# Projection chunks in another order, and attention set between them at a computed rate, in a one-core decoder layer

## The chip, the cores and the metric

One core of one Trainium2 chip runs the whole program. The metric is the device time of one execution in microseconds; the median of three runs of the kernel before is 1526.23 us (1516.66 to 1528.02).

## The reference

One layer of a decoder with two kinds of mixer, over a prompt of 2048 tokens and 64 new (sample) tokens. All shapes below are for the prompt.

```python
u, va, za, q, k, vb, zb = split(rms_norm(x) @ w_in)          # w_in 1024 x 3584
q, k = rms_norm per head                                       # 8 heads x 64
# mixer A: 4 channel groups of 128, chunks of 128 positions
a = rms_norm(u * (tril(w_s) @ rms_norm(va) + b_s)) * silu(za)
# mixer B: three dilated window patterns, r = 1, 4, 16, 129 keys each
o_r, lse_r = softmax attention of t to t - j*r, j = 0..128
b = rms_norm(sum_r softmax(lse)_r * o_r) * silu(zb)
h = x + concat(a, b) @ w_out
y = h + sigmoid(h @ w_ple_gate) * rms_norm(p @ w_ple)
```

The sample tokens do the same against a cache of 2048 keys and values per sequence.

## The kernel before

The projection is cut by columns into eight chunks. A chunk "A i" holds u, va and za of channel group i (384 columns); a chunk "B i" holds q, k, vb and zb of the head pair i (512 columns). `order` (L1251) lists them as A0 B0 B1 A1 B2 B3 A2 A3. Each chunk is a loop over 16 prompt tiles of 128 tokens and one sample tile (j from 0 to 16, L1284); a prompt tile is 24 matmuls (`gemm`, L433; operands are split into float16 halves, three products each). ScalarE (ACT) and VectorE (DVE) empty the result from PSUM (`psg`, three buffers; L475 to L491 for B, L565 to L571 for A), and GpSimd (POOL) scales it (L500 to L513, L581, L582). While a chunk runs, the weights of the next are loaded and split (`wprep`, L333); in the last chunk those of the three final products are (`wprep3`, L799; the low halves are L831 on VectorE).

Attention of a head pair needs its B chunk. `attn` (L642) cuts a pair into units. The first half of a unit is `scores` (L688): matmuls L698 and L699 into `pss`, a masked maximum on VectorE (L704), an exponential on ScalarE (L712), the float16 split on VectorE (L715, L716) and a transposing DMA to `pT` (L718). The second half is `stage_c` (L721): matmuls L739 to L741 with the values, and a row tile `rec` written to DRAM (L748 to L752). When a pair's last unit is through, `combine` (L755) runs once for each quarter of the tokens: it loads the three patterns' rows (`rl`, L760; three buffers) and the gates (`gzl`, L763), weighs and adds them on GpSimd (L776, L778, L781, L790, L792) with small VectorE steps between, and writes `catd` (L794). The four quarters follow each other in the same three buffers, and all of them need the last rows of pattern 3. The pairs use one buffer for their keys and queries (`kq`, L346), so pair i begins when pair i-1 is done.

The units are set between the projection's matmuls by `Pump` (L55). `tick` is called after each two matmuls and adds their planned nanoseconds times `rate` to a credit; units, each with a planned cost, are set while the credit is positive. The rate is 0.6 in every chunk (L1280) and 0.5 in the final stage (L1357). A unit's second half is due 8000 planned ns after its first. Before half of a B chunk, `pump.run` (L1343) sets what is left of the pair before.

The samples' attention (`all_samples`, L1229, four rounds of `sample`, L1063) is handed over at the end of chunk B3 (L1338) and is set only when no unit of a pair is left (`_step`, L97). A round multiplies cached keys by queries on GpSimd (L1126, 16 times: tiles `K` loaded at L1122 and `qB` at L1125, in the three buffers each that `pT` and `pc` use in attention), sums them on VectorE (L1127), transposes other keys on TensorE (L1106, L1111), and weighs values with `L1187` and `L1206`.

The final stage goes through the 16 prompt tiles: `p3_load` reads `catd` (L891), `halves_T` (L845) scales and splits it (L839, L861, L863) and transposes it by DMA (`Tc`, L862, L864), and `gemm2` (L867) multiplies by w_out, w_ple and w_ple_gate (L874). Tile 0 needs the first quarter of `combine` of pair 3.

Every engine works off its own list in the order in which a scheduler has put it. All DMAs here but a few small ones are issued from the one list of SP.

Of the kernel before, what the change touches and what calls it, by code (L numbers as in the profile page):

```python
# [24 lines left out]
NT = T // P  # L25
# [18 lines left out]
W_V = 4000.0  # L44
W_V3 = 3000.0
QK_LAG = 3000.0
P_LAG = 8000.0
MIX_LAG = 12000.0

# [86 lines left out]
def tile_hymba_gmlp_dilated_attn_step(  # L136
# [30 lines left out]
    drm = ctx.enter_context(tc.tile_pool(name="drm", bufs=1, space=DRAM))  # L167
    pump = Pump(3, P_LAG)
    uid = [0]

    def nm(s):
        uid[0] += 1
        return f"{s}_{uid[0]}"
# [259 lines left out]
    def gemm(j, wt, ncol):  # L433
        g = pst("g", 3)
        n = 0
        for kt in range(KT):
            w = wt[kt // 2]
            a, b = w[:, kt % 2, 0, :ncol], w[:, kt % 2, 1, :ncol]
            lh = xT[j][:, kt]
            for l, r in ((lh, a), (lh, b), (xT[j][:, KT + kt], a)) if j < NT else ((lh, a), (lh, b)):  # L440
                last_mm[0] = nc.tensor.matmul(g[:, :ncol], lhsT=l, rhs=r, start=(n == 0),  # L441
                                              stop=(n == (23 if j < NT else 15)))
                n += 1
                if n % 2 == 0:
                    pump.tick(2 * (ncol * 0.416 + 5))
        return g if j < NT else fold(g, ncol, "tmpA")
# [27 lines left out]

    def b_evac(G, q, g, sc):  # L475
        m = G["m"]
        g4 = g[:m, 0:256].rearrange("p (a d) -> p a d", d=HD)
        nc.scalar.activation(G["raw"][:m, q, :], g[:m, 0:256], AF.Copy)
        sq = wk.tile([P, 256], F32, name=nm("sq"), tag="sq", bufs=2)
        nc.scalar.activation(sq[:m], g[:m, 0:256], AF.Square)  # L480
        nc.vector.tensor_reduce(G["ss"][:m, q * 4:(q + 1) * 4], sq[:m].rearrange("p (a d) -> p a d", d=HD),
                                axis=AX.X, op=ALU.add)
        if m == P:
            gv = g[:, 256:384].rearrange("p (h d) -> p h d", h=2)
            vh = G["vv"][:, q, :, 0:64]
            nc.scalar.activation(vh, gv, AF.Copy, scale=VS)
            nc.vector.scalar_tensor_tensor(G["vv"][:, q, :, 65:129], gv, VS, vh, op0=ALU.mult, op1=ALU.subtract)
        nc.scalar.activation(G["vo"][:m, q, :], g[:m, 256:384], AF.Copy, scale=sc[:m, 1:2])
# [148 lines left out]
    vt = {}  # L637

    done = {}
    v_open = []  # L640

    def attn(hp, sc, grp):  # L642
        start = pump.now + QK_LAG
        qk2 = kq[hp]
        Q, KH, KL = qk2[:, 0:2], qk2[:, 2:4], qk2[:, 4:6]
        steps = []
        if grp is None:
            for c in range(0, 16, 2):
                steps.append((3, c // 4, [(c % 4 + s, False, slice(c + s, T, 16), slice(c + s, T, 16))
                                          for s in range(2)]))  # L650
        else:
            n = grp
            for j in range(4 * n, 4 * n + 4):
                steps.append((1, n, [(j % 4, j > 0, slice(j * P, (j + 1) * P),
                                      slice(max(j - 1, 0) * P, (j + 1) * P))]))
            for c in range(4):
                steps.append((2, n, [(c, n > 0, slice(n * 512 + c, (n + 1) * 512, 4),
                                      slice(max(n - 1, 0) * 512 + c, (n + 1) * 512, 4))]))
        rec = {}
        for pat, g, sub in steps:  # L660
            o = {}

            def first(pat=pat, g=g, sub=sub, o=o):
                if sub[0][0] == 0:
                    if pat != 1:
                        vload(hp, pat, g)
                    rec[pat] = wk.tile([P, 4, 2, RW], F32, name=nm("rec"), tag="rec", bufs=2)
                o["r"] = rec[pat]
                o["pT"], cost = scores(Q, KH, KL, o["r"], sub)
                return cost  # L670

            def second(pat=pat, g=g, sub=sub, o=o):
                with behind():
                    cost = stage_c(hp, pat, g, sub, o["r"], o["pT"])
                if pat == 1 and (sub[0][0] == 0 and g or sub[0][0] == 3 and g == 3):
                    v_open.pop(0)
                return cost
            pump.unit(start, first, second)
        if grp is None:
            for jg in range(4):  # L680
                def comb(jg=jg):
                    combine(hp, jg, sc)
                    done[hp] = jg == 3
                    return 0.0
                pump.unit(start, comb, None)
# [562 lines left out]
            nc.vector.tensor_scalar(gch[:, 2, :], gch[:, 1, :], cS, None, op0=ALU.mult)  # L1248
        gains.append(gch)

    order = [("A", 0), ("B", 0), ("B", 1), ("A", 1), ("B", 2), ("B", 3), ("A", 2), ("A", 3)]  # L1251

    room = wk.tile([P, 6, D], F32, name="room", tag="qk2", bufs=1)
    xst = []
# [18 lines left out]
    for ci, (kind, i) in enumerate(order):  # L1273
# [10 lines left out]
        for j in range(NT + 1):  # L1284
# [25 lines left out]
            if j % 4 == 0:  # L1310
                mk = b_group if kind == "B" else a_group
                G = mk(i, j // 4, 4, P) if j < NT else mk(i, 4, 1, TS)
            g = gemm(j, wt, ncol)
            if ci + 1 < len(order):
                for _ in range(1 if ci else FIRST_PREP[j]):
# [103 lines left out]
```

## Time and profile before

| | |
|---|---|
| median of 3 runs | 1526.23 us |
| the profiled execution's own time | 1526.24 us |
| its span on the trace | 1524.5 us |
| TensorE (PE) busy | 1361.5 us, 89% |
| VectorE (DVE) busy | 1160.8 us, 76% |
| ScalarE (ACT) busy | 725.9 us, 48% |
| GpSimd (POOL) busy | 538.1 us, 35% |
| mean granted TensorE clock | 0.959 |

An engine's share is a mean over nine stages that have different limits, so it says little alone. The trace can be asked for the busy time of each engine in given stretches, for instructions in order of time, and for groups of instructions by line.

### The profile page before, as it was taken

To read this page: it belongs to the slowest core of one execution; us is meant where nothing else is said; L and a number is where in the kernel's file an instruction comes from. 1 tells how busy PE (TensorE), PEld (TensorE's weight loads), DVE (VectorE), ACT (ScalarE), POOL (GpSimd) and SP (SyncE) were. 2 spreads that over 40 slices of the span, in tenths; PEclk is the share of its full clock that TensorE was granted. 3 is DMA by queue.
4 is the path that set the end of the run, shared out by engine and by line. 5 is a ranking of instruction groups with operands and counts; after the bars stand their busy time and mean duration, and the time that the engine had idled before them with its cause. 6 is when DMAs were issued, how large, how long until landed. Compare 5 with 4: busy or idle time off the path is not lost. (4 is left out here: it accounts for less than half of the span.)

```text
span 1524.5 us, 26216 instructions
## 1 busy us (share of the span) xinstructions
PE 1361.5 (89%) x8280; PEld 693.3 (45%) x8280; DVE 1160.8 (76%) x3775; ACT 725.9 (48%) x2083; POOL 538.1 (35%) x547
## 2 busy tenths in 40 slices
PE   2989988997899988899888986788998999899998
PEld 1544544554555434455445643443343344344443
DVE  6777887588988789876999899879756675675555
ACT  6675666565656446655665544754322122221222
POOL 7123122234543654322344356643232330330101
PEclk9999999999999999999999998799999999999999
DMA  7983698588965457977697587876899799796432
GB/s 195 238 181 97 131 176 171 119 176 183 210 155 126 132 120 161 215 142 164 151 211 161 127 207 222 230 204 157 208 224 251 188 255 240 194 242 155 105 94 64
DMA packets 591436, 266.06 MB, mean 175 GB/s; under 512 B 338337, under 2 KB 568801, under 8 KB 591297
## 3 DMA queue, kind: packets, MB, share of 16 engines
q1 hardware_dynamic: 589312, 262.73, 75.4%
q0 software_dynamic: 1984, 1.66, 0.7%
q8 instruction: 65, 1.06, 0.3%
q14 instruction: 75, 0.61, 0.1%
HBM read 134.56 MB, written 48.01 MB: 120 GB/s over the span
## 5 line engine op out<-in xcount | busy, mean ns | idle before, releaser
L441 PE MATMUL psg<-wt,xT 128*128 128x512 f16 (+1 forms) x3072 | 649.6, 367 | 36.5 <-DVE agz L571 15.2
L441 PEld LDWEIGHTS <-xT 128*128 128x128 f16 x3072 | 309.9, 102 | 331.3 <-issue 60.1
L712 ACT ACTIVATE sm<-sm,rec,psc 128x256 f32<-128x256 f32 (+1 forms) x384 | 185.1, 546 | 129.4 <-DVE rec L708 103.1
L698 PE MATMUL pss<-qk 128*128 128x256 f16 (+1 forms) x384 | 132.0, 355 | 31.2 <-DMA qk<-qkc 17.2
L1126 POOL TENSOR_TENSOR K<-K,qB 96x512 f32<-96x512 f32 x64 | 88.4, 1386 | 165.8 <-DMA K<-in_cache_k_dram 70.3
L704 DVE CUSTOM_DVE_ANT_0 sm<-pss,mask 128x256 f32<-128x256 f32 (+1 forms) x384 | 122.7, 360 | 29.2 <-PE pss L699 28.1
L699 PE MATMUL pss<-qk 128*128 128x256 f16 (+1 forms) x384 | 132.8, 358 | 0.0
L874 PEld LDWEIGHTS <-Th 128*128 128x128 f16 x800 | 77.1, 99 | 109.9 <-issue 21.5
L874 PEld LDWEIGHTS <-Tc 128*128 128x128 f16 x800 | 76.4, 98 | 110.6 <-issue 19.9
L716 DVE TENSOR_TENSOR pc<-sm,pc 128x512 f16<-128x512 f32 (+1 forms) x160 | 119.0, 744 | 1.6
L963 POOL TENSOR_TENSOR tg<-tg,x 128x1024 f32<-128x1024 f32 (+1 forms) x16 | 37.6, 2347 | 183.4 <-DVE tg L962 160.4
L874 PE MATMUL psg<-w,Th 128*128 128x512 f16 x400 | 97.6, 387 | 1.2 <-DMA Th<-hl 0.5
L861 ACT ACTIVATE hl<-x,sm 128x1024 f16<-128x1024 f32 (+1 forms) x17 | 19.5, 1147 | 166.0 <-DVE sm L842 140.7
L715 DVE CAST pc<-sm 128x512 f16<-128x512 f32 (+1 forms) x160 | 80.5, 503 | 23.3 <-ACT sm L712 21.3
L874 PE MATMUL psg<-w,Tc 128*128 128x512 f16 x400 | 95.6, 379 | 2.8 <-DMA Tc<-hl 2.8
L874 PE MATMUL pss<-w,Th 128*128 128x512 f16 x400 | 94.9, 379 | 0.0
L874 PE MATMUL pss<-w,Tc 128*128 128x512 f16 x400 | 93.8, 379 | 0.0
L1127 DVE TENSOR_REDUCE blk<-K 96x8 f32<-96x512 f32 x64 | 43.0, 678 | 61.2 <-POOL K L1126 61.1
L776 POOL TENSOR_TENSOR rl<-rl,sm 128x520 f32<-128x520 f32 x48 | 55.7, 1187 | 82.9 <-ACT sm L772 80.0
L739 PEld LDWEIGHTS <-pT 128*128 128x128 f16 x600 | 57.3, 98 | 52.7 <-DMA pT<-pc 43.9
L513 POOL TENSOR_TENSOR gz<-gz,gch 128x512 f32<-128x512 f32 x16 | 20.8, 1301 | 168.9 <-DVE gz L491 83.9
L744 ACT ACTIVATE rec<-pso 128x130 f32<-128x130 f32 (+1 forms) x160 | 44.4, 295 | 46.7 <-PE pso L741 45.3
(324 smaller groups left out, 2649.5 us busy)
## 6 DMA issues: line engine op xcount, KB each, us to landing
K<-in_cache_k_dram SPq DMA_DIRECT2D x64, 192.0 KB
qB<-qd SPq DMA_DIRECT2D x64, 192.0 KB
V<-in_cache_v_dram SPq DMA_DIRECT2D x64, 192.0 KB
vt<-vscr SPq DMA_DIRECT2D x32, 258.0 KB
K<-in_cache_k_dram SPq DMA_DIRECT2D x32, 256.0 KB
V<-in_cache_v_dram SPq DMA_DIRECT2D x32, 256.0 KB
cat<-catd SPq DMA_DIRECT2D x16, 512.0 KB
x<-in_x_prompt_dram SPq DMA_DIRECT2D x16, 512.0 KB
```

Source lines behind the costliest of these rows:

```text
L441: last_mm[0] = nc.tensor.matmul(g[:, :ncol], lhsT=l, rhs=r, start=(n == 0), stop=(n == (23 if j < NT else 15)))
L698: nc.tensor.matmul(pss[:, s, h], lhsT=Q[:, h, qs], rhs=KH[:, h, ks], start=True, stop=False)
L699: nc.tensor.matmul(pss[:, s, h], lhsT=Q[:, h, qs], rhs=KL[:, h, ks], start=False, stop=True)
L704: nc.vector.tensor_tensor_reduce(sm4[:, s, h], pss[:, s, h], mk, 1.0, -3.0e38, op0=ALU.add, op1=ALU.max, accum_out=mx[:, i:i + 1])
L712: nc.scalar.activation(sm4[:, s, h], sm4[:, s, h], AF.Exp, bias=r[:, sl + s, h, HD + 1:HD + 2], scale=psc)
L715: nc.vector.tensor_copy(pc[:, :n], smv)
L716: nc.vector.tensor_tensor(pc[:, n:2 * n], smv, pc[:, :n], op=ALU.subtract)
L739: nc.tensor.matmul(po[:, s, h, 0:65], lhsT=H, rhs=v[:, vs_, a:a + 65], start=(bi == 0), stop=False)
L744: nc.scalar.activation(r[:, sl:sl + ns, :, 0:65], po[:, :ns, :, 0:65], AF.Copy)
L776: nc.gpsimd.tensor_tensor(ti, ti, e[:, i, :].unsqueeze(2).to_broadcast([P, 8, 65]), op=ALU.mult)
L874: last_mm[0] = nc.tensor.matmul(gs[hf], lhsT=o[part][:, kt], rhs=w[:, kt % 2, half, :], start=(n[hf] == 0), stop=(n[hf] == (3 if m == P el ...
L1126: nc.gpsimd.tensor_tensor(K3, K3, qB, op=ALU.mult)
```

## The change

The order of chunks becomes A0 B0 B1 A1 B2 A2 B3 A3: chunk B3 moves one place back, behind A2. The rate is no longer 0.6 but is set anew for each tile by `pace`: planned work left of the current pair (`left`, at first 33800 ns) over the planned time from this tile to the pair's end less 9000 ns, held between 0.2 and 0.8. A pair's end is tile 7 of the next B chunk, and for pair 3 tile 10 of the last chunk. The samples are still handed over at the end of B3 and set when no unit is left. No operation is added or removed.

```diff
@@ -44,6 +44,9 @@
 W_V = 4000.0
 W_V3 = 3000.0
 QK_LAG = 3000.0
+
+PAIR_NS = 33800.0
+TAIL = 9000.0
 P_LAG = 8000.0
 MIX_LAG = 12000.0
@@ -637,10 +640,12 @@
     done = {}
+    left = {}
     v_open = []
 
     def attn(hp, sc, grp):
         start = pump.now + QK_LAG
+        left.setdefault(hp, PAIR_NS)
         qk2 = kq[hp]
@@ -667,11 +672,13 @@
                 o["pT"], cost = scores(Q, KH, KL, o["r"], sub)
+                left[hp] -= cost
                 return cost
 
             def second(pat=pat, g=g, sub=sub, o=o):
                 with behind():
                     cost = stage_c(hp, pat, g, sub, o["r"], o["pT"])
+                left[hp] -= cost
@@ -1248,7 +1255,19 @@
-    order = [("A", 0), ("B", 0), ("B", 1), ("A", 1), ("B", 2), ("B", 3), ("A", 2), ("A", 3)]
+    order = [("A", 0), ("B", 0), ("B", 1), ("A", 1), ("B", 2), ("A", 2), ("B", 3), ("A", 3)]
+
+    tile_ns = [24 * ((512 if kind == "B" else 384) * 0.416 + 5) for kind, _ in order]
+    place = lambda ci, j: sum(t * (NT + 0.7) for t in tile_ns[:ci]) + j * tile_ns[ci]
+
+    ends = [place(order.index(("B", i + 1)), 7) if i < 3 else place(len(order) - 1, 10) for i in range(4)]
+
+    def pace(ci, j):
+        hp = next((h for h in range(4) if not done.get(h)), None)
+        if hp is None or hp not in left:
+            return 0.6
+        return min(max(left[hp] / max(ends[hp] - TAIL - place(ci, j), 1000.0), 0.2), 0.8)
@@ -1310,6 +1329,7 @@
                 G = mk(i, j // 4, 4, P) if j < NT else mk(i, 4, 1, TS)
+            pump.rate = pace(ci, j)
             g = gemm(j, wt, ncol)
```

In the rows below, lines of the changed kernel are 3 to 7 higher than those of the kernel before (L704 is L711 there, L741 is L748, L874 is L881).

The first place is VectorE in the first half of chunk B2, from the result of tile 5 to that of tile 6 (L491, L494 in the changed kernel). `gz` is the gate of the projection, `raw` and `qkc` the keys and queries, `rl` what `combine` has loaded, `pss` the scores, `pc` the split probabilities. The kernel before:

```order
L547 TENSOR_TENSOR qkc_7189<-raw_6953,qkc_7189 128x2x64
L783 TENSOR_REDUCE sm_6608<-rl_6588 128x8
L787 SCALAR_TENSOR_TENSOR sm_6610<-sm_6608,sm_6610 128x8
L183 TENSOR_SCALAR sm_6614<-sm_6610 128x8
...
L481 TENSOR_REDUCE sm_7200<-sq_7490 128x4
L487 SCALAR_TENSOR_TENSOR v_1242_7202<-psg_7448,v_1242_7202 128x2x64
...
L491 SCALAR_TENSOR_TENSOR gz_7204<-th_7496,psg_7448 128x128
```

VectorE between the same two results of the changed kernel:

```order
L711 ISA sm_7325,sm_7326<-pss_7324,mask 128x128
L711 ISA sm_7326 128x1
...
L715 TENSOR_SCALAR rec_7323<-sm_7326,nsc 128x2
L722 CAST pc_7336<-sm_7325 128x256
L711 ISA sm_7342,sm_7343<-pss_7341,mask 128x256
...
L775 TENSOR_TENSOR sm_7094<-sm_7094,rl_7089 128x8
...
L490 SCALAR_TENSOR_TENSOR v_1201_6989<-psg_7308,v_1201_6989 128x2x64
...
L494 SCALAR_TENSOR_TENSOR gz_6991<-th_7408,psg_7308 128x128
```

Scores stand where only `combine` of the pair before stood; the instructions L711 count 88, 172, 72, 124, 72, 132 and 108 (of 192 for a pair) from stage to stage behind A0, where L704 counts 88, 176, 120, 76, 180, 128 and 0.

The second place is TensorE at the last attention matmul. `pT` holds the last probabilities, `xT` and `xTs` the projection's inputs, `Tp` and `Tc` the transposed rows of p and of `catd` in the final stage. The kernel before:

```order
L741 LDWEIGHTS pT_11985
L741 MATMUL pso_12109<-vt_11883,pT_11985 128x65
L1087 MATMUL pst_12498<-ident,blk 128x64
L1088 MATMUL pst_12498<-ident,blk 128x64
L441 LDWEIGHTS xT_1140
L441 MATMUL psg_12468<-wt_10087,xT_1140 128x384
...
L1133 MATMUL pst_13804<-ident,blk 128x96
L874 LDWEIGHTS Tp_13650
...
L874 LDWEIGHTS Tc_13638
L874 MATMUL pss_13795<-w_2329_13285,Tc_13638 128x512
```

The changed kernel at its last attention matmul:

```order
L748 LDWEIGHTS pT_12775
L748 MATMUL pso_12894<-vt_12638,pT_12775 128x65
L1113 MATMUL pst_13449<-ident,K_13155 128x128 x4
L444 LDWEIGHTS xTs
L444 MATMUL psg_13528<-wt_10936,xTs 128x384
...
L1113 MATMUL pst_13674<-ident,K_13447 128x128 x4
L881 LDWEIGHTS Tp_13499
...
L881 LDWEIGHTS Tc_13487
L881 MATMUL psg_13664<-w_2229_12861,Tc_13487 128x512
```

Between the last attention matmul and the first that reads `Tc` stand 490 matmuls before the change and 28 after it (8 of the projection, 12 transposes of sample keys, 8 that read `Tp`).

The third place is SP's list behind that point, from the last rows of pattern 3 (`r3d`) to the transposing DMA of tile 0. The kernel before:

```order
L748 DMA r3d_114<-rec_11885 128x528
...
L794 DMA catd_118<-gzl_9711 128x4x128
L760 DMA rl_12128<-r3d_114 128x4x132
...
L1122 DMA K_2319_13251<-in_cache_k_dram 96x4x128
L760 DMA rl_12168<-r2d_110 128x4x132
...
L794 DMA catd_115<-gzl_12130 128x4x128
...
L862 DMA_TRANSPOSE Tc_13638<-hl_2395_13636 128x8x128
```

SP's list of the changed kernel:

```order
L755 DMA r3d_114<-rec_12640 128x528
...
L767 DMA rl_12940<-r3d_114 128x4x132
L1129 DMA K_2416_13718<-in_cache_k_dram 96x4x128
...
L1129 DMA K_2447_13861<-in_cache_k_dram 96x4x128
...
L1183 DMA V_2517_14175<-in_cache_v_dram 96x4x128
L801 DMA catd_115<-gzl_12942 128x4x128
...
L898 DMA cat_13414<-catd_115 128x1024
...
L869 DMA_TRANSPOSE Tc_13487<-hl_2348_13485 128x8x128
```

In the changed kernel the write of the first quarter of `catd` still stands behind the loads of the first sample round (nine `K` tiles and then values, the last of them in buffers that the sixteenth multiplication frees), and the load of tile 0 right behind it; the previous pair's last `catd` write (`gzl_9711` before) no longer stands between the write of `r3d` and its reading.

## Rows read from the trace of the kernel before

**Rows 1.** Stretches by stage: length; PE, PEld, DVE, ACT, POOL busy; clock; DMA.
```profile
core 0 of [0], span 1524.5 us
115.00:228.00 113.00, 105.84 (x671) 53.97 (x670) 90.00 (x324) 67.26 (x207) 29.95 (x41) 0.98 0.63 134
228.00:382.00 154.00, 139.38 (x995) 75.56 (x994) 115.02 (x457) 88.76 (x262) 47.18 (x58) 0.96 0.75 163
382.00:498.00 116.00, 107.09 (x824) 66.11 (x822) 101.06 (x370) 69.24 (x221) 51.27 (x47) 0.93 0.71 160
498.00:627.00 129.00, 111.36 (x647) 54.80 (x646) 111.91 (x371) 64.37 (x201) 67.39 (x73) 0.93 0.65 145
627.00:782.00 155.00, 143.29 (x1022) 78.14 (x1021) 125.25 (x472) 93.55 (x274) 46.38 (x57) 0.97 0.82 170
782.00:906.00 124.00, 110.33 (x869) 68.93 (x867) 109.30 (x390) 68.19 (x227) 58.43 (x63) 0.96 0.77 175
906.00:1019.00 113.00, 84.86 (x456) 46.20 (x454) 96.90 (x264) 64.70 (x208) 69.57 (x61) 0.88 0.75 214
1019.00:1525.00 506.00, 480.97 (x2378) 204.96 (x2376) 327.85 (x811) 131.97 (x294) 124.20 (x83) 0.99 0.80 183
```

**Rows 2.** The same stretches, L704 alone: length; DVE busy (instructions); clock; DMA.
```profile
115.00:228.00 113.00, 15.48 (x88) 0.98 0.63 134
228.00:382.00 154.00, 28.09 (x176) 0.96 0.75 163
382.00:498.00 116.00, 18.29 (x120) 0.93 0.71 160
498.00:627.00 129.00, 13.41 (x76) 0.93 0.65 145
627.00:782.00 155.00, 29.28 (x183) 0.97 0.82 170
782.00:906.00 124.00, 19.54 (x126) 0.96 0.77 175
```

**Rows 3.** The last projection stage, L831 alone: length; DVE busy; clock; DMA.
```profile
906.00:1019.00 113.00, 18.98 (x20) 0.88 0.75 214
```

**Rows 4.** TensorE in order of time: start, duration, line, operands, count.
```profile
898.99 0.20 PE L741 MATMUL pso<-vt,pT 128*128 128x65 f16 x1
...
1020.12 1.24 PE L874 MATMUL pss<-w,Tc 128*128 128x512 f16 x5
```

**Rows 5.** SP's DMA issues in order of time.
```profile
900.79 0.47 SPq L748 DMA_DIRECT2D r3d<-rec  x1
...
915.81 0.60 SPq L760 DMA_DIRECT2D rl<-r3d  x1
...
958.85 0.57 SPq L794 DMA_DIRECT2D catd<-gzl  x1
```

**Rows 6.** GpSimd in order of time, first quarter of pair 3's combine.
```profile
922.73 3.13 POOL L776 TENSOR_TENSOR rl<-rl,sm 128x520 f32<-128x520 f32 x3 [1.44 <-ACT sm L772]
925.82 2.94 POOL L1126 TENSOR_TENSOR K<-K,qB 96x512 f32<-96x512 f32 x2
...
954.06 1.18 POOL L792 TENSOR_TENSOR gzl<-rl,gzl 128x512 f32<-128x512 f32 x1
```

**Rows 7.** VectorE in order of time, at the final stage's first row maximum.
```profile
1008.22 1.21 DVE L839 TENSOR_REDUCE sm<-cat 128x1 f32<-128x1024 f32 x1
```

**Rows 8.** VectorE in order of time, one step of the root twice.
```profile
904.31 0.15 DVE L184 TENSOR_TENSOR sm<-sm 128x4 f32<-128x4 f32 x1
...
932.52 1.21 DVE L184 TENSOR_TENSOR sm<-sm 128x4 f32<-128x4 f32 x1
```

**Rows 9.** Groups by line: busy us, mean ns of one, idle before.
```profile
L1111 PE MATMUL pso<-KT,blk 128*32 128x512 f32 x64 | 31.4, 647 | 0.0
L1106 PE MATMUL pst<-ident,K 128*128 128x128 f32 x128 | 20.9, 289 | 10.6 <-ACT KT L1116 8.0 <-DVE sb L611 1.8 <-DVE ua L611 0.8
```

## The prediction

> **What bounds the kernel now.** I read the engines by stage first, then where attention lies in those stages, then the passage from projection to final stage in order of time, engine by engine.
>
> The stretches [rows 1] run from the last VectorE result of one chunk's prompt tiles to that of the next: B0, B1, A1, B2, B3, A2, A3, and the final stage. The reader is to see two limits. In the final stage TensorE is busy 480.97 of 506 us; nothing but its own work sets the time there. In the projection TensorE is busy for 75 to 94% and VectorE for 75 to 88%; no engine is full, and each stage loses time to waits between the two. A3 stands out: no attention in it, 113 us long, TensorE busy for 84.86 us and at a mean granted clock of 0.88, so 24% of it, some 27 us, at 1.2 GHz in place of 2.4 GHz. Its 28 us of idle TensorE are the largest of any of these stretches.
>
> The scores [rows 2] tell how uneven attention is: 88, 176, 120, 76, 183, 126 and, in A3, none. B1 and B3, with the most, last 154 and 155 us; B0, with half of it, 113 us. The stage lengths follow the counts: (154 - 113) / (176 - 88) = 0.466 us for one score. I take 0.45.
>
> **The change, part by part.** Nothing is added or removed, so the sum has three terms: what even spreading saves in the projection, what the later end of pair 3's attention costs at the passage, and what the samples' later start moves onto a full TensorE.
>
> *Spreading.* With 0.45 us a score, a B stage without attention comes to 73 to 75 us (113 - 40, 154 - 79, 155 - 82), an A stage to 62 to 67 (116 - 54, 124 - 57) [rows 1, 2]. Two stages lie over this: B2 by 129 - 34 - 74 = 21 us, A3 by 113 - 65 = 48 us. B2 holds nearly all of pair 1's combine, and has the most GpSimd time of the B stages, 67.39 us. A3 holds weight splitting for the final stage, the first sample round and pair 3's combine. The changed kernel's counts, from its order, are B1 172, A1 72, B2 124, A2 72, B3 132, A3 108. Priced the same way: 74 + 77 = 151, 65 + 32 = 97, 74 + 56 = 130, 97, 74 + 59 = 133, 65 + 49 = 114; sum 722 us. Before, the same six stages are 154 + 116 + 129 + 155 + 124 + 113 = 791 us. So 69 us go if neither excess is left. They can be left: 21 us in B2, 21 us in B3 (it now holds pair 2's combine, as B2 does pair 1's), and in A3 about 20 us, the VectorE time of the weight splitting [rows 3]. That is 62 us, and leaves a gain of 7. Attention itself is not made cheaper, it only changes neighbours, so I see no loss here. Between 7 and 69 I take the middle, 38 us.
>
> *The passage.* Before, the last attention matmul ends at 899 us and the first one that reads tile 0's `Tc` starts at 1020.12 us [rows 4]. Between them lies a whole chunk, 490 matmuls, so whatever combine needs is hidden. After the change 28 matmuls lie there. This is the place that decides. The chain from the one to the other can be timed in the trace of before, because it runs there too, with other work of TensorE over it:
> - from the last attention matmul to the first GpSimd step of the first quarter: 922.73 - 898.99 = 23.7 us. In it, `r3d` is written at 900.79 and read at 915.81 [rows 5], 15 us of which some 12 are the wait for the previous pair's last quarter. That wait goes. In its place VectorE has the 16 low halves of w_out in front of combine's first step, 16 x 18.98 / 20 = 15 us [rows 3], and the first seven sums of the sample round. I take 23; ends 12 (nothing in place of the wait) and 32 (all of it, with a load in the way).
> - GpSimd's steps to the end of L792: 954.06 + 1.18 - 922.73 = 32.5 us, shared with six sample multiplications and six steps of A3 [rows 6]. After: eight multiplications, each waiting for a load, and no step of a chunk. I take 25; ends 23 and 34.
> - to the issue of the `catd` write: 958.85 - 955.24 = 3.6 us [rows 5, 6], because SP's list stands at other loads. After the change it stands behind the values of the sample round, freed by the sixteenth multiplication. I take 2; ends 1 and 4.
> - `catd` landing and tile 0 being read: two DMAs one after the other. The read of `r3d` took from 915.81 to at most 922.73 with three small steps behind it [rows 5, 6], so 4 to 6 for the two at the least load; I take 4.
> - from the row maximum to the matmul: 1020.12 - 1008.22 = 11.9 us [rows 4, 7], with VectorE and ScalarE emptying tiles at the same time. I take 8; ends 7 and 12.
>
> Sum 62 us; ends 47 and 88. A3 ends at 1019 - 38 = 981, its last attention matmul about 2 us behind, so tile 0 starts at 981 + 2 + 62 = 1045 in place of 1020 us: 25 us late. TensorE has nothing to fill this with, since its list has only those 28 matmuls before `Tc`.
>
> A rule of the Trainium skill speaks against the change here. The same 128x4 step of a root took 0.15 us at one place and 1.21 us beside GpSimd's work at another [rows 8]. SBUF — State Buffer, section "SBUF: two separate sides", says that VectorE and GpSimd share a port pair that is locked for a whole instruction, so that a VectorE step with two SBUF inputs waits until a GpSimd step that reads SBUF is over; these rows agree. By that rule some ten small steps of combine, each beside a multiplication, would add 10 x 1.06, about 11 us, to the 25; the sum here leaves it out, as the 32.5 us of the trace hold such waits already.
>
> *Samples.* The first round began inside A3. Its TensorE part there, 20 transposes and 8 sums by the two orders, goes into the full final stage: 20 x 20.9 / 128 + 8 x 31.4 / 64 = 3.3 + 3.9 = 7 us [rows 9]. The last round still ends well before the last tiles: its last value matmul stands in block 27 of the 37 blocks of 48 matmuls L874 that its order makes, before in block 25, so no round has to be set in one piece at the end. Cost of that: none.
>
> *Sum.* 25 + 7 = 32 us on the span: 1524.5 + 32 = 1556.5. The profiled execution's own time is 1.7 us over its span and equals the median, so 1558 us.
>
> **Rivals.**
> 1. *The passage is covered or short* (faster). Place: tile 0's `Tc`. If TensorE reaches it as late as the operands, the 25 us become -36 (981 + 2 + 1 against 1020), and the time 1526 - 36 + 7 = 1497. For: the scheduler may have put combine late only because it had time; the trace's chain shares its engines with a chunk. Against: TensorE's list, fixed at build, has 28 matmuls there, some 5 us of work, and SP's list has nine key loads before the `catd` write. It decides from the chain's length: with the middle gain the change is even at a chain of 30 us, and 1% faster at 15. With the full gain of 69 us these become 61 and 46.
> 2. *The two cancel*. A chain at its short end, 47 us, and a gain of 50 give 1019 - 50 + 2 + 47 = 1018, 2 us early, plus 7: 1531 us. For: once TensorE stands, nothing else asks VectorE and GpSimd for time. Against: A3 now carries 108 scores on top of the weight splitting, and a stage with both is in no row.
> 3. *Worse than forecast*. A gain of 7 and a chain of 88: 1019 - 7 + 2 + 88 = 1102, 82 late, plus 7: 1615 us. Both ends at once is unlikely.
> 4. *The change doesn't do what it says*: the rate, held at 0.2 to 0.8, might leave attention where it was. The counts from the order rule that out.
>
> The clock is no rival of its own. A3's 0.88 goes with its idle TensorE [rows 1]; a standstill at the passage would leave the first matmuls behind it at 1.2 GHz. By the Trainium skill (TensorE: Matmul & The Clock Gate, section "What's actually happening") the idle state is the slow one; A3's row agrees. If a few microseconds are lost so, they are inside the ends above.
>
> **How the numbers follow.** The gain's half width is 31 us, the chain's 15 down and 26 up. Taken together as independent: 34 down, 40 up, so 1524 to 1598. I widen the low end to 1510 to take in part of rival 1 and cut the high end to 1595. Forecast and rival 3, slower than 1541.5 us: 0.60. Rival 2, within 1% (1510.9 to 1541.5; about what a measurement of this kernel tells from no change): 0.23. Rival 1: 0.17.
>
> **What would show it.** Right: A1 and A2 near 100 us, B1 as before, the end of A3 near 981 us, then a standstill of TensorE of some 50 us with `Tc` as releaser and a granted clock well under 1 in it, the first quarter's `catd` write behind sixteen multiplications, and a final stage of some 515 us from there. Wrong: a standstill under 30 us, or an A3 over 135 us, which would move the loss from the passage into the stage itself; or samples that end so late that the last tiles wait for them.

## The result

The changed kernel takes 1567.87 us (median of 4 runs, 1564.05 to 1568.51), the kernel before beside it 1525.81 us: a ratio of 1.0282 with a 95% interval of 1.0249 to 1.0315. It is slower by 42 us. The profiled execution took 1568.36 us with a span of 1566.4 us.

The stretches of the changed kernel from chunk to chunk follow; they answer to [rows 1] (columns as there). The order is now B0, B1, A1, B2, A2, B3, A3, then the passage, then the final stage from tile 0's first `Tc` matmul.

```profile
117.00:227.00 110.00, 103.16 (x665) 53.10 (x664) 88.90 (x318) 66.13 (x206) 29.43 (x40) 1.00 0.64 135
227.00:382.00 155.00, 141.81 (x985) 75.80 (x984) 116.46 (x455) 88.86 (x263) 47.12 (x58) 0.92 0.76 160
382.00:484.00 102.00, 91.87 (x694) 55.73 (x692) 88.93 (x309) 56.25 (x184) 52.45 (x49) 0.95 0.71 152
484.00:622.00 138.00, 125.70 (x802) 64.87 (x801) 106.65 (x398) 75.33 (x234) 54.20 (x61) 0.95 0.67 145
622.00:720.00 98.00, 87.84 (x662) 53.58 (x660) 84.14 (x289) 53.56 (x182) 38.65 (x39) 0.97 0.64 140
720.00:862.00 142.00, 127.70 (x824) 66.64 (x823) 109.94 (x415) 76.81 (x237) 54.47 (x60) 0.96 0.67 143
862.00:978.00 116.00, 104.65 (x796) 64.76 (x793) 95.76 (x350) 67.49 (x227) 44.75 (x53) 0.96 0.80 185
978.00:1052.00 74.00, 5.20 (x16) 2.48 (x17) 40.66 (x107) 27.46 (x65) 41.53 (x32) 0.52 0.83 227
1052.00:1566.00 514.00, 493.46 (x2415) 208.39 (x2413) 332.88 (x817) 133.63 (x298) 129.53 (x88) 0.98 0.78 184
```

The reader is to see three things. The projection is shorter: A3 ends at 978 us, 40.6 us before the 1018.8 us of the kernel before. Then comes a stretch that the kernel before does not have, 74 us in which TensorE is busy for 5.2 us, at a granted clock of 0.52, that is nearly all at 1.2 GHz. And the final stage is some 10 us longer (514.2 against 504.4 us from the first `Tc` matmul to the end). 32 us of tile 0 and 10 us of final stage are the 42 us.

The scores of five of these stretches (L711, L704 before; they answer to [rows 2]) are the counts of the prediction, within 4:

```profile
382.00:484.00 102.00, 13.73 (x76) 0.95 0.71 152
484.00:622.00 138.00, 18.22 (x120) 0.95 0.67 145
622.00:720.00 98.00, 12.96 (x72) 0.97 0.64 140
720.00:862.00 142.00, 20.50 (x132) 0.96 0.67 143
862.00:978.00 116.00, 16.13 (x108) 0.96 0.80 185
```

TensorE in order of time at the passage (it answers to [rows 4]; the number in brackets is the idle time ahead, with what ended it):

```profile
974.85 0.20 PE L748 MATMUL pso<-vt,pT 128*128 128x65 f16 x1
...
989.87 1.12 PE L1113 MATMUL pst<-ident,K 128*128 128x128 f32 x4 [12.36 <-ACT KT L1123]
...
1049.03 1.89 PE L881 MATMUL psg<-w,Tp 128*128 128x512 f16 x4 [56.19 <-DMA Tp<-hl]
...
1052.24 1.03 PE L881 MATMUL psg<-w,Tc 128*128 128x512 f16 x4
```

From the last attention matmul (ends 975.05) to the first `Tc` matmul there are 77.2 us. Of the two long waits in them the first is for ScalarE, which empties transposes of sample keys; the second, 56 us, is for tile 0's operands. The profile names `Tp` and not `Tc` as its releaser: SP issues `Tp`'s transposing DMAs in turn with those of `Tc`, and the first `Tc` matmul follows 3 us later. The chain itself is read on the other engines. ScalarE, then SP, VectorE and GpSimd of the changed kernel, each in order of time:

```profile
977.69 8.05 ACT L837 ACTIVATE w<-w3st,sm 128x512 f16<-128x512 f32 x13
985.65 0.36 ACT L751 ACTIVATE rec<-pso 128x260 f32<-128x260 f32 x1
```

```profile
979.78 7.05 SPq L813 DMA_DIRECT2D w3st<-in_w_ple_gate_dram  x8
986.87 3.31 SPq L1129 DMA_DIRECT2D K<-in_cache_k_dram  x2
...
994.91 3.22 SPq L755 DMA_DIRECT2D r3d<-rec  x1
...
1003.00 0.36 SPq L767 DMA_DIRECT2D rl<-r3d  x1
...
1033.09 0.38 SPq L801 DMA_DIRECT2D catd<-gzl  x1
...
1035.93 0.50 SPq L898 DMA_DIRECT2D cat<-catd  x1
```

```profile
985.60 7.36 DVE L838 SCALAR_TENSOR_TENSOR w<-w3st,sm,w 128x512 f16<-128x512 f32 x11
...
1007.45 0.17 DVE L775 TENSOR_TENSOR sm<-sm,rl 128x8 f32<-128x8 f32 x1 [2.85 <-DMA rl<-r3d]
...
1020.42 1.22 DVE L792 TENSOR_TENSOR sm<-rl 128x8 f32<-128x8 f32 x1 [0.56 <-POOL rl L785]
...
1026.16 0.17 DVE L188 TENSOR_TENSOR sm<-sm,sm 128x8 f32<-128x8 f32 x1
...
1039.89 1.22 DVE L846 TENSOR_REDUCE sm<-cat 128x1 f32<-128x1024 f32 x1 [2.65 <-DMA cat<-catd]
```

```profile
1009.33 3.08 POOL L783 TENSOR_TENSOR rl<-rl,sm 128x520 f32<-128x520 f32 x3
...
1020.35 1.26 POOL L1133 TENSOR_TENSOR K<-K,qB 96x512 f32<-96x512 f32 x1
...
1031.89 1.18 POOL L799 TENSOR_TENSOR gzl<-rl,gzl 128x512 f32<-128x512 f32 x1
```

The last row tile `rec` is ready on TensorE at 975 us, but ScalarE has 13 high halves of w_out in front of it and copies it at 985.65. SP then writes it only at 994.91, since eight loads of w_gate (to 986.83) and loads of the samples' keys and queries (to 994.81) stand before it, and reads it back at 1003.00. From there the chain goes as in [rows 6]: GpSimd's steps with eight multiplications between, `catd`, tile 0.

### The profile page after: what moved, and what is told of

It reads as the page before. It is cut to its first block, busy times and chain, and to the rows that moved or that the text cites. A ratio compares the mean times of both kernels' runs of the same rounds, so it can differ in the third digit from the quotient of the medians.

```text
span 1566.4 us, 26159 instructions
## 1 busy us (share of the span) xinstructions
PE 1361.7 (87%) x8280; PEld 690.3 (44%) x8280; DVE 1148.1 (73%) x3775; ACT 723.9 (46%) x2083; POOL 536.5 (34%) x547
## 4 chain that ended last, share of the span: by engine, by line
PE 47%; DVE 22%; DMA 15%; issue 5%; ACT 5%; POOL 3%; SPq 2%; POOLq 0%; ACTq 0%; DVEq 0%
PE psg L444 17%; PE psg L881 9%; PE pss L881 9%; PE pss L705 3%; PE pss L706 3%; DMA qB<-qd 2%; DVE sm L711 2%; DMA pT<-pc 2%; PE pso L1213 2%; DVE rec L715 2%; DVE pc L722 2%; DMA rl<-r3d 2%; DVE w L838 1%; DMA K<-in_cache_k_dram 1%; DVE pc L723 1%
## 5 line engine op out<-in xcount | busy, mean ns | idle before, releaser
L444 PE MATMUL psg<-wt,xT 128*128 128x384 f16 (+1 forms) x3072 | 647.9, 365 | 20.1 <-DMA xT<-xhl 11.1
L444 PEld LDWEIGHTS <-xT 128*128 128x128 f16 x3072 | 306.4, 101 | 302.8 <-issue 39.4
L705 PE MATMUL pss<-qk 128*128 128x256 f16 (+1 forms) x384 | 131.4, 354 | 24.5 <-DVE sm L711 13.3
L711 DVE CUSTOM_DVE_ANT_0 sm<-pss,mask 128x256 f32<-128x256 f32 (+1 forms) x384 | 122.8, 358 | 37.1 <-PE pss L706 35.5
L881 PEld LDWEIGHTS <-Tc 128*128 128x128 f16 x800 | 75.7, 98 | 118.3 <-issue 35.2
L881 PEld LDWEIGHTS <-Th 128*128 128x128 f16 x800 | 76.8, 98 | 101.9 <-issue 11.3
L881 PE MATMUL psg<-w,Tc 128*128 128x512 f16 x400 | 98.1, 383 | 0.0
L881 PE MATMUL psg<-w,Th 128*128 128x512 f16 x400 | 94.6, 379 | 1.1 <-DMA Th<-hl 1.1
L881 PE MATMUL pss<-w,Tc 128*128 128x512 f16 x400 | 94.5, 379 | 0.0
L881 PE MATMUL pss<-w,Th 128*128 128x512 f16 x400 | 94.1, 379 | 0.0
L881 PE MATMUL psg<-w,Tp 128*128 128x512 f16 x100 | 28.5, 395 | 56.2 <-DMA Tp<-hl 56.2
```

Source lines behind the costliest of these rows:

```text
L705: nc.tensor.matmul(pss[:, s, h], lhsT=Q[:, h, qs], rhs=KH[:, h, ks], start=True, stop=False)
L711: nc.vector.tensor_tensor_reduce(sm4[:, s, h], pss[:, s, h], mk, 1.0, -3.0e38, op0=ALU.add, op1=ALU.max, accum_out=mx[:, i:i + 1])
L881: last_mm[0] = nc.tensor.matmul(gs[hf], lhsT=o[part][:, kt], rhs=w[:, kt % 2, half, :], start=(n[hf] == 0), stop=(n[hf] == (3 if m == P el ...
```

## The experiments

The lines of the experiments lie a few above those of the changed kernel. "Behind" means order in an engine's list only: no wait is added. Ratios are to the kernel before in the same set; the changed kernel's is 1.0282. Theory A at the start: work of others ("visitors") in the chain's lists makes it long. Theory B: the chain's own steps do.

**The samples behind the first quarter.** The loads (SP) and multiplications (GpSimd) of the sample round are set behind the first quarter's last multiplication and its write of `catd`.

```diff
+        if hp == 3 and jg == 0:
+            gate.extend([mul, put])
...
+                with after(*gate):
                     nc.sync.dma_start(K3, ck[b, 0:1536, cs]...)
+                with after(*gate):
                     nc.sync.dma_start(qB, src...)
                     nc.gpsimd.tensor_tensor(K3, K3, qB, op=ALU.mult)
```

> The first sample round's loads and multiplications are set behind the first quarter's combine of pair 3 in the lists of SP and POOL (order only, no added wait). Theory A (visitors: other work standing in the passage's lists makes the 77 us from the last attention matmul to the first Tc matmul): the key loads that held SP from 986.87 to 994.8 in front of the write of r3d go (8 us), and eight multiplications of about 1.26 us go from between POOL's combine steps (10 us); the chain falls to about 59 us and the time to about 1550 us. Theory B (combine's own steps and their waits make it): the chain stays over 70 us and the time within 5 us of 1568.

Measured: 1572.73 us (1.0280, 1.0255 to 1.0305). The chain did shorten, to 62.2 us, and `Tc` started at 1037.5 us; nothing of it reached the time. The final stage took 529.7 us in place of 514.2. Its row beside the one above:

```profile
1037.00:1567.00 530.00, 494.18 (x2415) 208.57 (x2413) 345.95 (x825) 133.28 (x298) 146.10 (x99) 0.98 0.82 190
```

TensorE's work is the same (494 and 493 us); the time in which it is not busy rose from 20.5 to 35.8 us. VectorE and GpSimd have 13 and 17 us more to do there, and TensorE waits, for instance, 6.6 us for tile 0's `Th`, whose split on VectorE has sums of sample products among the steps in front of it. A part of the gain was lost before `Tc`: the first quarter's write of `catd` came 26 us earlier (1007.07 against 1033.09), `Tc` only 14.7, since the samples' loads now stood in SP's list among tile 0's own steps. So this work costs about as much behind the standstill as it did in it. Theory A was right on the chain and wrong on the time.

**The weights behind.** The halves of w_out go behind the last `rec` and combine's first small steps, the loads of w_gate behind combine's first loads; in the text the halves come two tiles later.

```diff
-LAST_PREP = [1, 1, 2, 2, 2, 3, 3, 3, 3, 3, 3, 3, 3, 3, 3, 2, 2]
+LAST_PREP = [1, 1, 2, 2, 2, 3, 3, 3, 3, 0, 0, 3, 3, 3, 3, 3, 3]
...
+                with after(late["ld"]) if label == "g" else nullcontext():
                     nc.sync.dma_start(t, src...)
...
+                    with after(late["rec"], late["sub"]) if label == "o" else nullcontext():
                         nc.scalar.activation(w[:, k2, 0, :], ...)
```

> The preparation of w_out is set behind the last row tile rec on ACT and behind combine's first small steps on DVE, and the eight loads of w_gate behind combine's first loads on SP (order only; in the program text the halves of w_out come two tiles later). Theory A: rec comes about 1 us after the last attention matmul in place of 10.7 us, and 7 us of w_gate issues leave SP's list in front of r3d; the chain falls from 77 to about 62 us, the time to about 1553 us. Theory B: r3d then waits for something else (the key loads), the chain stays over 70 us, time within 5 us of 1568.

Measured: 1562.05 us (1.0202, 1.0175 to 1.0229), chain 69.0 us. SP of this run:

```profile
977.00 0.61 SPq L757 DMA_DIRECT2D r3d<-rec  x1
...
982.69 1.71 SPq L769 DMA_DIRECT2D rl<-r3d  x1
```

`rec` was copied within 0.1 us of the last matmul and `r3d` was written 18 us earlier. GpSimd's first step, at 999.3 in place of 1009.3, came 23.3 us behind the last matmul and not 34.3, so the weights were in the way there. Of the 18 us, 8 are left at `Tc`: the halves of w_out now stand between combine's steps. By the ratios it is worth 0.8%, 12 us, of the 15 expected. One of the halves shows what VectorE can lose beside GpSimd:

```profile
997.35 6.82 DVE L844 SCALAR_TENSOR_TENSOR w<-w3st,sm,w 128x512 f16<-128x512 f32 x1
```

Others of them take 0.74 us in this run; here GpSimd's steps followed each other without a gap from 996.71 to 1005.33.

**The order alone**, with the old rate, **and the rate alone**, with the old order.

```diff
-            pump.rate = pace(ci, j)
```
```diff
-... ("B", 2), ("A", 2), ("B", 3), ("A", 3)]
+... ("B", 2), ("B", 3), ("A", 2), ("A", 3)]
```

> New order of chunks, with the old rate of 0.6. If the order alone puts pair 3's attention at the end of the projection (its list has 20 matmuls between the last attention matmul and the first Tc), the standstill stays and the time is 1568 within 10 us; priced at 0.45 us a score the six stages sum to 723 us, as with the computed rate. Rival: the computed rate is what costs (attention held back), then this is near 1530.

> Old order of chunks, with the computed rate. Its list has 222 matmuls between the last attention matmul and the first Tc, 182 of them projection, some 40 us of TensorE's work. By the same prices the stages save 27 to 39 us; with the last attention matmul some 45 us before the end of A3 and a chain of 62 to 77 us tile 0 starts near 1010 to 1020: time 1515 to 1535. Rival: if spreading saves nothing without the new order, A3 has 48 scores more than before and the time is 1540 to 1560.

Measured: the order alone 1592.34 us (1.0408, 1.0393 to 1.0424), the rate alone 1551.64 us (1.0142, 1.0107 to 1.0178). The order alone lies above its expectation and far above its rival; the rate alone missed its expectation and fell into the range of its rival. Each half by itself is slower than the kernel before, and on the new order the computed rate is worth 1.3%, some 19 us. The standstill is the same without it (chain 79.2 us), but A3 ends at 996 us and not at 978. Stretches B2 and B3 of the order alone, all engines, then L711:

```profile
504.00:641.00 137.00, 115.07 (x656) 55.21 (x655) 116.74 (x370) 64.03 (x202) 69.04 (x74) 0.91 0.65 138
753.00:881.00 128.00, 105.97 (x623) 51.60 (x622) 111.14 (x364) 59.02 (x191) 66.05 (x70) 0.95 0.60 136
```

```profile
504.00:641.00 137.00, 13.61 (x77) 0.91 0.65 138
753.00:881.00 128.00, 13.23 (x76) 0.95 0.60 136
```

B2 takes 137 us with 77 scores, and 138 us with 120 in the changed kernel. So 0.45 us a score is no price in a stage that holds a whole combine (GpSimd 69 us): B2 did not get shorter when scores left it. By 0.45 us these two should take 109 and 108 us; the other four stages sum to 503 us where the prices say 507. That the combine sets the length there is an inference; no run took it out. The rate helped because it took scores out of A1 and A2 (120.4 and 112.0 us here, 101.8 and 97.6 there) and put them where they cost less: 1 us for 43 scores in B2, 15 us for 56 in B3.

With the old order, B3 has 180 scores and a combine and takes 168 us, A3 with 56 scores 127 us (rate alone, all engines):

```profile
625.00:793.00 168.00, 147.20 (x995) 76.78 (x994) 138.05 (x504) 92.05 (x276) 64.92 (x72) 0.90 0.79 169
901.00:1028.00 127.00, 98.04 (x589) 56.60 (x587) 92.05 (x316) 74.42 (x243) 64.87 (x65) 0.88 0.80 212
```

The two chunks B2 and B3 follow each other there, so a pair that must end before half of the next B chunk has no A chunk to spread into. A3 ends at 1027.8, 9 us later than before, and `Tc` starts at 1039.0, 19 us later: a short standstill lies between, 11 us with TensorE busy for 4.0.

**Samples and weights both behind.**

> The edits of the two runs with the samples behind and the weights behind, together. Theory A' (what is pushed out of the standstill is paid in the final stage, on a full TensorE): the chain falls to about 54 us (77 - 15 - 8), the final stage grows by about 15 us as with the samples alone, time 1550 to 1560 us. Rival (the chain alone sets the end): time about 1568 - 23 = 1545 us or less.

Measured: 1565.65 us (1.0284, 1.0253 to 1.0315), above either expectation. The chain is 64.5 us, no shorter than with the samples alone behind (62.2), so the two gains do not add, and the final stage again took 529 us.

**Attention kept in its place**: each projection matmul goes behind the last attention matmul of pair 3 that the program text has set before it (`last_c`).

```diff
+                with after(*last_c):
                     last_mm[0] = nc.tensor.matmul(g[:, :ncol], lhsT=l, rhs=r, ...)
```

> In A3 the projection's matmuls are set behind the attention matmuls that the program text has before them (order only, in TensorE's list): 148 projection matmuls, 6.2 tiles, then stand between the last attention matmul and the first Tc, where 8 stood. Theory C (what costs is the place of the last attention matmul in TensorE's list): it comes 6 tiles of about 5 to 7 us earlier, near 940 to 950 us, and with a chain of 62 to 77 us tile 0 starts at 1005 to 1025: time 1520 to 1540 us. Rival (TensorE then waits in A3 for probabilities not yet transposed): A3 grows by 15 us or more beyond its 116 us and the time stays over 1550 us.

Measured: 1575.57 us (1.0327, 1.0294 to 1.0360); the rival. Stretches B3 and A3:

```profile
722.00:878.00 156.00, 131.24 (x869) 68.27 (x868) 118.70 (x452) 82.53 (x249) 61.71 (x67) 0.92 0.68 144
878.00:1047.00 169.00, 119.35 (x759) 69.75 (x758) 116.86 (x376) 89.06 (x274) 66.35 (x71) 0.78 0.74 185
```

Though 148 projection matmuls were put behind it, the last attention matmul ran at 987 us, 12 us later than in the changed kernel: an earlier place in TensorE's list did not make it earlier. TensorE is not busy for 50 of A3's 169 us, against 11 of 116 in the changed kernel. Its longest waits in A3 (us in all, times, longest):

```profile
PE psg L445 <- DVE agz L576: 14.0, 2, 10.0
PE pss L707 <- DVE sm L713: 11.3, 4, 5.7
PE pso L748 <- DMA pT<-pc: 11.0, 4, 5.8
```

Some 22 us are waits for attention (its maximum, its transposing DMA), and 14 us are the projection's own, for VectorE to empty a result. In the changed kernel the scheduler had set projection where attention was not ready.

**Pattern 3 first.** Only pattern 3 is needed by all quarters; for pair 3 its units go ahead of the last group's, and three quarters of combine directly behind them. Group 2's values of pattern 2 are loaded once more.

```diff
-                    attn(i, sc, jg)
-                    if jg == 3:
-                        attn(i, sc, None)
+                    if jg == 3:
+                        for g in (3, None) if i < 3 else (None, 3):
+                            attn(i, sc, g)
+                    else:
+                        attn(i, sc, jg)
```

> For pair 3 the units of pattern 3 are set ahead of the last group's units of patterns 1 and 2, and the first three quarters of combine right behind them; the values of group 2 of pattern 2 are loaded once more. Tile 0's chain then begins at the last matmul of pattern 3, behind which 158 projection matmuls (6.6 tiles, some 45 us) stand before the first Tc, where 8 stood. Theory C: chain start near 935 us, chain 62 to 77 us from there, tile 0 at 1000 to 1012: time 1505 to 1530 us. Rival: combine in the middle of A3 shares VectorE, GpSimd and SP with attention and projection, the chain takes 100 us, tile 0 at 1035 or later: time over 1545 us.

Measured: 1546.87 us (1.0153, 1.0127 to 1.0179): the largest single gain, and yet the rival's number. The chain did begin early, `r3d` being written at 941.7 us, but the first quarter then took long. GpSimd:

```profile
950.09 3.79 POOL L785 TENSOR_TENSOR rl<-rl,sm 128x520 f32<-128x520 f32 x3 [4.21 <-ACT sm L781]
...
1005.43 1.17 POOL L801 TENSOR_TENSOR gzl<-rl,gzl 128x512 f32<-128x512 f32 x1
```

56.5 us from the first step's start to the last one's end, against 23.7 in the changed kernel: eight multiplications and the constants of the samples, steps of A3, and on VectorE the halves of w_out between combine's small steps. `Tc` started at 1032.0.

**The same with attention in place, samples and weights behind.**

> Pattern 3 first, the projection's matmuls of A3 behind attention, the samples behind the first quarter's combine and the weights behind: 260 projection matmuls (10.8 tiles, over 60 us) stand between the last matmul of pattern 3 and the first Tc. Theory C: the standstill is gone (under 15 us), A3 ends between 980 and 1000 us and sets the start of tile 0; final stage 505 to 525 us: time 1495 to 1520 us, below both kernels. Rival: A3 grows by what the standstill loses; time 1530 to 1560 us.

Measured: 1571.9 us (1.0311, 1.0282 to 1.0340), above either expectation. A3 takes 157 us, against 129 with pattern 3 first alone; holding attention in place lengthens it again.

**Pattern 3 first with the samples behind, then also with the weights behind.**

> Pattern 3 first as before, and the sample round (its constants, loads, multiplications) behind the first quarter's combine in the lists of SP, POOL and DVE. With pattern 3 first alone, r3d was written at 941.7 us, POOL began the first quarter at 950, and its last step ended only at 1006.6, with eight multiplications of the samples, their sums and constants between; Tc followed at 1032. Theory D (that stretch of 57 us is visitors): the last step ends at 975 to 985 us, Tc starts at 1000 to 1010, and as the samples then start on a TensorE that has the final stage to do, that stage takes 515 to 530 in place of 512 us: time 1517 to 1540 us, about 1528. Rival (repaid in full, as with the samples behind in the first set): 1542 us or more.

> The same, and the preparation of w_out and w_gate set later as in the run with the weights behind. There it was worth 6 to 13 us of time, since rec and r3d came earlier; here the row tile of pattern 3 is written in the middle of A3, before that work, so theory D expects nothing from the front of the chain and 0 to 5 us from the VectorE time of the halves (15 us) that then stands less in front of combine: 1515 to 1540 us. Rival: the halves, later, now stand in front of tile 0's first matmul: 5 to 15 us slower than the run beside it.

Measured: 1549.35 us (1.0158, 1.0096 to 1.0219) and 1548.07 us (1.0149, 1.0097 to 1.0200). The first run's GpSimd, at the same two steps:

```profile
953.57 4.15 POOL L787 TENSOR_TENSOR rl<-rl,sm 128x520 f32<-128x520 f32 x3 [1.29 <-ACT sm L783]
...
979.22 1.17 POOL L803 TENSOR_TENSOR gzl<-rl,gzl 128x512 f32<-128x512 f32 x1
```

27 us in place of 56.5: theory D was right that the rest was visitors. `Tc` started at 1014.7 us, later than theory D had it but 5 us earlier than in the kernel before, and the time did not move: the final stage took 532.1 us. That is the rival's number. The weights behind changed nothing that the two intervals would show, neither the gain nor the loss that was expected.

**Samples handed over with tile 3, then tile 2, of the final stage.**

```diff
-                    elif i == 3:
-                        pump.back.append(all_samples())
...
             p3_cat(new)
+            if new == 3:
+                frozen.append(1)
+                pump.back.append(all_samples())
```

> Pattern 3 first, and the sample rounds handed over only with tile 3 of the final stage (order only, behind tile 3's transposes; the last value matmul of the samples then stands in block 31.4 of 37.5 of the final stage's matmuls, where 27.5 stood). With the samples right behind the first quarter's combine, Tc started at 1014.7 us, but 34 us lay between the last step of that combine (980.4) and Tc, and TensorE then stood 29 us in the final stage, 12.5 of them in its first 100 us. Theory E (the samples cost where they meet combine, the weight halves and the tail of A3, that is from 980 to 1110 us, and little later): Tc starts at 995 to 1003 us, TensorE stands under 20 us behind it, its work there is about 497 us: time 1508 to 1525 us, about 1515, at or below the kernel before. Rival (what is pushed out is repaid wherever it goes): 1538 us or more.

> As the run before, but the sample rounds are handed over with tile 2 of the final stage; their last value matmul then stands in block 29.5 of 37.5, two blocks of about 13.6 us earlier. In the run before, Tc started at 1002.2 us and the final stage took 550 us: about 503 us of TensorE's work (480 in the kernel before; 16 sums and 32 transposes of the first sample round, with its values, are on the full TensorE now), 13.3 us of waiting for the sample tile's Tc near the end and some 31 us of other waits. Theory F (what was left of the gain is eaten by those two): without the wait at the end the final stage takes 525 to 537 us: time 1528 to 1541, about 1534, below the changed kernel by over 25 us and not below the kernel before. Rival (the waits only move): 1548 us or more.

Measured: 1552.46 us (1.0189, 1.0164 to 1.0215) and 1544.8 us (1.0139, 1.0118 to 1.0161). `Tc` started at 1002.2 and 1000.0 us, as expected, 18 and 20 us before the kernel before; both are slower than it all the same. With tile 3, TensorE waits for the sample tile near the end:

```profile
1495.34 2.29 PE L890 MATMUL psg<-w,Tc 128*128 128x512 f16 x5 [13.26 <-DMA Tc<-hl]
```

With tile 2 that is gone, and another wait as long stands at the samples' first round. TensorE, then VectorE, ScalarE and SP in front of it:

```profile
1103.19 3.17 PE L890 MATMUL psg<-w,Tc 128*128 128x512 f16 x7 [12.90 <-DMA Tc<-hl]
```

```profile
1090.07 5.10 DVE L782 TENSOR_TENSOR sm<-sm,rl 128x8 f32<-128x8 f32 x3
1095.34 1.13 ACT L875 ACTIVATE hl<-cat,sm 128x1024 f16<-128x1024 f32 x1
1100.05 1.27 SPq L876 DMA_TRANSPOSE Tc<-hl  x1
```

Three small steps of a combine, 0.34 us together in the changed kernel, took 5.10 us beside GpSimd's work, which had hardly a gap from 1089.67 to 1094.98 (two multiplications of the samples and a step on an output tile). ScalarE's split of the tile, `hl`, stands behind an exponential that waited 6.4 us for them, and the transposing DMA followed 3.6 us behind the split, with two sample loads and a wait of 2.0 us for VectorE between. It is the passage's own mechanism at another tile. Theory E was right on `Tc` and wrong on what follows: with tile 3 TensorE was not busy for 47 us of the final stage, where it had under 20. Theory F half held; 1544.8 lies between its range and the rival's.

All of it in one table (us, from the profiled execution of each; "not busy" is the length less TensorE's busy time in the final stage):

| kernel | first `Tc` | final stage | TensorE busy | not busy |
|---|---|---|---|---|
| before | 1020.1 | 504.4 | 479.9 | 24.5 |
| changed | 1052.2 | 514.2 | 493.3 | 20.9 |
| samples behind | 1037.5 | 529.7 | 493.7 | 36.0 |
| pattern 3 first | 1032.0 | 511.6 | 488.5 | 23.1 |
| pattern 3 first, samples behind | 1014.7 | 532.1 | 496.7 | 35.4 |
| pattern 3 first, samples from tile 2 | 1000.0 | 544.5 | 507.5 | 37.0 |

Wherever the samples are pushed back, what is won at `Tc` is lost behind it: 14.7 us won and 15.5 lost on the changed kernel, 17.3 and 20.5 with pattern 3 first, 32.0 and 32.9 from tile 2. It is lost as waits and as TensorE's work. Of the 27.6 us of work that the last row has over the first, 14.4 are 16 sums and 32 transposes of the first round; the rest is mainly the same matmuls taking longer, at a granted clock of 0.96 in that stage in place of 0.99. The kernel before set that round in A3, whose TensorE had 28 us to spare [rows 1]. None of these versions beats it.

## Why the prediction was right, and where it was off

- **Direction and place**: right. The standstill is where it was put, with tile 0's operands as releaser; 1566.4 us of span against 1556.5. The 10 us between them are four misses, two of either sign: the chain 15 longer and the samples 3 dearer, A3's end 3 and the last attention matmul 5 earlier than forecast.
- **Spreading, 38 us** (ends 7 to 69): A3 ended 40.6 us earlier. The six stages took 750.9 us where the prices gave 722; so 29 of the assumed 62 us of excess were left. In B2 and B3, with 21 us each in the prediction, 8 and 10 were left (28 and 20 with the order alone). In A3, with 20, only 2 were: of the 20 low halves of weights that the prediction put there, 16 (12.2 us of VectorE) ran behind A3's end, in the passage, where it had counted those of w_out a second time. The other 9 us stand in B1, A1 and A2, where it had none. That the gain came out within 3 us is luck: 38 was the middle of a wide range, and the price behind it failed; 0.45 us a score did not hold in a stage with a whole combine.
- **The passage, 62 us** (ends 47 to 88): 77.2. By pieces, predicted and measured: 23 and 34.3; 25 and 23.7; 2 and 0; 4 and 6.8; 8 and 12.4. The step that was mis-sized is the first, "23 (12 to 32)". It had VectorE's low halves of w_out in it, and they were there. It did not have the high halves in ScalarE's list, behind which `rec` came 10.6 us after the last matmul, and it had a load in the way on SP only in its upper end, where the loads of w_gate and of the samples held the write for 8.9 us more. Two runs show these as the cause: with the weights behind `r3d` is written 18 us earlier and the piece is 23.3 us; with the samples alone behind `r3d` is written right behind `rec`, at 984.84.
- **Tile 0 late by 25 us**: 32.1. Attention ended 3 us before A3's last result and not 2 us behind it, the chain took 15 more.
- **Samples, 7 us**: the final stage grew by 9.8. The number of sums was wrong: 16 moved, not 8. L1118 there is 64 matmuls and 34.7 us, before (L1111) 48 and 26.0; the 20 transposes cost 3.1 us. Some 4 us less waiting took a part back.
- **Rivals**: the first would have needed a chain of 30 us; the shortest that a run measured from the last attention matmul, where that ends pattern 3, was 62.2, and with pattern 3 first no less than 57 lay between the last write of `r3d` and `Tc`. The second needed both a gain of 50 and a chain of 47. The third was not reached at either end.
- **VectorE beside GpSimd**: L792 at 1020.42 lies beside the multiplication of 1020.35 to 1021.61 and takes 1.22 us, but the steps of the root stand between multiplications and take 0.15 to 0.17. So one step of that quarter was held up, by about 1 us, where the prediction named a price of 11 us and left it out of its sum. It had that price from a rule of the Trainium skill (SBUF — State Buffer, section "SBUF: two separate sides"): a VectorE step with two inputs in SBUF and a GpSimd step that reads SBUF wait for each other. The rows agree with the rule and not with the price. The steps of 6.82 and 5.10 us in the experiments agree with it too: where GpSimd's steps leave no gap, one wait cost more than all of that quarter's.

What stays open: whether the samples' first round could be given a place in the new order where TensorE has time. Its buffer is that of pair 3's keys and queries, so it can't start before pair 3's scores end; a version with room of its own was not tried. Open too is what sets the length of a stage with a whole combine.

## What to carry to other kernels

When work is spread to fill an idle stage, ask first what that idle stage was hiding: here it covered a chain of 60 to 80 us and gave the samples' first round free time on TensorE, together more than the spreading won. A chain on in-order lists is lengthened by the strangers in these lists (77 us here, 62 without the samples), so list, engine by engine, every step that is ready sooner, loads included, before pricing the chain. And a standstill that is removed by pushing others' work back is worth only what that work does not cost at its new place.

## What was not expected of the hardware

- The restart behind the standstill was cheap. The stretch shows a granted clock of 0.52, nearly all of it at 1.2 GHz, and the first four `Tp` matmuls took 0.47 us each (1.89 for 4), but those of `Tc` behind them 0.26: by an estimate from these rows some 2 us in all.
- SP's issues are not of one length: the same write of `r3d` held SP for 0.47 us in the kernel before and for 3.22 us in the changed one, where the loads of w_gate and of the samples' keys had just been issued and the DMA engines were busy for 0.83 of the stretch. What of it is their load was not tested.
